# RMSNorm with SiLU on one core: gamma's row fetched as eight transfers of 1 KB in place of one of 8 KB

## The chip, the cores and the metric

The kernel runs on one NeuronCore of a Trainium2 chip. The metric is device time in microseconds; three runs of the kernel before gave 316.78 to 316.95 with a median of 316.93. Durations below come from one profiled execution of it. PE is the matrix engine, DVE the vector engine, ACT the scalar engine, SP the engine that only issues transfers here; "ACTq" and "SPq" are the instruction queues of ACT and SP where they issue a DMA.

## The reference

For x of 8 x 1024 x 2048 float32 (8192 rows of 2048), gamma of 2048 and eps = 1e-5:

```
rms = sqrt(mean(x**2, axis=-1) + eps)
out = gamma * x / rms
out = out * (1 / (1 + exp(-out)))
```

## The kernel before

The 8192 rows are cut into 16 blocks of 512 rows. A block is one SBUF tile `xt` of 128 partitions x 8192 float32 (4 MB): each partition holds J = 4 rows of 2048, which lie next to each other in memory. The pool holds six such tiles (BUFS = 6), and a block is computed in place: it is loaded into its tile, squared, scaled, put through SiLU and stored from the same tile. So load b + 6 needs the tile of block b to be stored.

Loads are issued by ACT (line 54) and stores by SP (line 102), one transfer of 4 MB each. The program order on each engine is written out by hand (`manual_schedule`). Per block b:

- squares: sums of squares of the four rows, one or two of them on ACT (line 65, `squares_scalar`), the others on DVE (line 73, `squares_vector`, whose elementwise output goes to the PSUM tile `junk_v` and is not used);
- `root` on ACT (line 82) gives the rms and `invert` on DVE (line 87) its reciprocal;
- `multiply` on DVE (line 92): four instructions, x * rstd * g;
- `silu` on ACT (line 98): two instructions, then the store.

The squares of block b + 1 stand between the multiply and the SiLU of block b, or before both, according to b. The load of block b + 3 (from block 6 on) is issued by ACT behind the first squares of block b + 1. The last block is multiplied by gamma alone (line 155), and its SiLU takes the reciprocal as a scale (line 157).

Before the loop stands the start-up (lines 106 to 118), which the change touches. ACT issues load 0. DVE fills `ones` and `eps_t`. ACT runs one small activation (line 109). SP issues the fetch of gamma into row 0 of the tile `g` (line 110). PE spreads that row over the 128 partitions: four matmuls (line 113) of a row of ones by 512 columns of g write `junk_v` in PSUM. ACT issues load 1. DVE copies `junk_v` to `g` (line 115). ACT then reads one column of `junk_v` (line 116, which makes ACT wait for DVE's copy), and only behind that, in ACT's program order, are loads 2 to 5 issued (lines 117 and 118). The squares of block 0 come next on both engines.

Of the kernel before, what the change touches and what calls it, by code (L numbers as in the profile page):

```python
# [1 line left out]

# [4 lines left out]

ACT = mybir.ActivationFunctionType
ALU = mybir.AluOpType


@with_exitstack
def kernel(
    ctx: ExitStack,
    tc: tile.TileContext,
    x: bass.AP,
    gamma: bass.AP,
    eps: bass.AP,
    out: bass.AP,
):  # L20

    nc = tc.nc
    P = nc.NUM_PARTITIONS
    f32 = mybir.dt.float32
    x2 = x.flatten_outer_dims()
    o2 = out.flatten_outer_dims()  # L30
    n, d = x2.shape
    J = 4
    BUFS = 6
    nblk = n // (P * J)
    xb = x2.rearrange("(b p j) d -> b p (j d)", p=P, j=J)
    ob = o2.rearrange("(b p j) d -> b p (j d)", p=P, j=J)

    singles = ctx.enter_context(tc.tile_pool(name="singles", bufs=1))
    pool = ctx.enter_context(tc.tile_pool(name="pool", bufs=BUFS))
    small = ctx.enter_context(tc.tile_pool(name="small", bufs=2))  # L40
    psum = ctx.enter_context(tc.tile_pool(name="psum", bufs=1, space=bass.MemoryType.PSUM))

    Q = 4
    w = d // Q
    g = singles.tile([P, d], f32)
    eps_t = singles.tile([P, 1], f32)
    ones = singles.tile([P, P], f32)
    junk_a = psum.tile([P, d], f32, name="junk_a")
    junk_v = psum.tile([P, d], f32, name="junk_v")
    blocks, sss, rmss, rstds = {}, {}, {}, {}  # L50

    def load(b):
        xt = pool.tile([P, J * d], f32, name="xt")
        nc.scalar.dma_start(out=xt, in_=xb[b])  # L54
        blocks[b] = xt

    def row(b, j):
        return blocks[b][:, j * d:(j + 1) * d]

    def squares_scalar(b, loads=()):  # L60


        sss[b] = small.tile([P, J], f32, name="ss")
        for j in range(share(b)):
            nc.scalar.activation(out=junk_a, in_=row(b, j), func=ACT.Square,  # L65
                                 accum_out=sss[b][:, j:j + 1])
            if j == 0:
                for s in loads:
                    load(s)

    def squares_vector(b):
        for j in range(share(b), J):
            nc.vector.tensor_tensor_reduce(  # L73
                out=junk_v, in0=row(b, j), in1=row(b, j), scale=1.0, scalar=0.0,
                op0=ALU.mult, op1=ALU.add, accum_out=sss[b][:, j:j + 1])

    def share(b):
        return 1 if 4 <= b <= 12 and b % 2 == 0 else 2

    def root(b):  # L80
        rms = small.tile([P, J], f32, name="rms")
        nc.scalar.activation(out=rms, in_=sss.pop(b), func=ACT.Sqrt, scale=1.0 / d, bias=eps_t)  # L82
        rmss[b] = rms

    def invert(b):
        rstd = small.tile([P, J], f32, name="rstd")
        nc.vector.reciprocal(out=rstd, in_=rmss.pop(b))  # L87
        rstds[b] = rstd

    def multiply(b):  # L90
        for j in range(J):
            nc.vector.scalar_tensor_tensor(out=row(b, j), in0=row(b, j), scalar=rstds[b][:, j:j + 1],  # L92
                                           in1=g, op0=ALU.mult, op1=ALU.mult)

    def silu(b):
        for h in range(0, J, 2):
            cols = slice(h * d, (h + 2) * d)
            nc.scalar.activation(out=blocks[b][:, cols], in_=blocks[b][:, cols], func=ACT.Silu)  # L98
        store(b)

    def store(b):
        nc.sync.dma_start(out=ob[b], in_=blocks[b])

    with tc.manual_schedule():

        load(0)
        nc.vector.memset(ones, 1.0)  # L107
        nc.vector.memset(eps_t, float(eps))
        nc.scalar.activation(out=junk_a[:, 0:1], in_=ones[:, 0:1], func=ACT.Square)  # L109
        nc.sync.dma_start(out=g[0:1, :], in_=bass.AP(tensor=gamma.tensor, offset=gamma.offset, ap=[[d, 1], [1, d]]))  # L110
        for c in range(Q):
            cols = slice(c * w, (c + 1) * w)
            nc.tensor.matmul(junk_v[:, cols], ones[0:1, :], g[0:1, cols], start=True, stop=True)  # L113
        load(1)
        nc.vector.tensor_copy(out=g, in_=junk_v)  # L115
        nc.scalar.copy(out=junk_a[:, 0:1], in_=junk_v[:, d - 1:d])  # L116
        for b in range(2, BUFS):
            load(b)

        last = nblk - 1
        SOON = 3
        squares_scalar(0)
        squares_vector(0)
        root(0)
        invert(0)
        for b in range(last):
            loads = [b + 3] if BUFS <= b + 3 < nblk else []
            if b < SOON:  # L130
                multiply(b)
                squares_scalar(b + 1, loads)
                silu(b)
                squares_vector(b + 1)
                root(b + 1)
            elif b < last - 1:
                squares_scalar(b + 1, loads)
                squares_vector(b + 1)
                root(b + 1)
                multiply(b)  # L140
                silu(b)
            else:
                multiply(b)
                squares_scalar(b + 1)
                silu(b)
                squares_vector(b + 1)
                root(b + 1)
            if b + 1 < last:
                invert(b + 1)


        for j in range(J):
            if j == J // 2:
                invert(last)
            nc.vector.tensor_mul(out=row(last, j), in0=row(last, j), in1=g)  # L155
        for j in range(J):
            nc.scalar.activation(out=row(last, j), in_=row(last, j), func=ACT.Silu,  # L157
                                 scale=rstds[last][:, j:j + 1])
        store(last)


# [1 line left out]
_INS = ['x', 'gamma', 'eps']  # L163
_OUTS = [((8, 1024, 2048), 'float32')]

_NUMBERS = {'eps': 9.999999747378752e-06}


# [26 lines left out]
```

## Time and profile before

| what | value |
|---|---|
| median of 3 runs | 316.93 us (316.78 to 316.95) |
| span of the profiled execution, first to last instruction | 315.1 us |
| time around the span in that execution | not given by its page; the median of the runs is 1.8 us above the span |
| DVE busy | 235.3 us, 75% of the span |
| ACT busy | 213.9 us, 68% |
| PE busy | 7.2 us, 2% |
| bytes moved | 134.24 MB, 426 GB/s over the span |
| granted PE clock | 1.000 |
| load, from issue to landing, median of 16 | 38.7 us |
| store, the same | 29.0 us |

The span is the time from the first to the last instruction of the execution. The page cuts it into 40 slices of 7.9 us and gives for each the busy tenths of every engine and of the 16 DMA engines that all transfers share. A row of the timeline has the start, the duration, the engine, the line, the operation, its tiles and in brackets the idle time of the engine ahead of it and what ended that. Besides, the trace has a record of each DMA packet with its start, duration, queue and bytes. In these records the loads are on queue q10, and the stores and gamma on q1.

### The profile page before, as it was taken

How to read it: one execution, taken by the hardware profiler on the slowest of the kernel's cores; microseconds unless marked ns; L12 is line 12 of the kernel's file. 1: busy time of each engine (PE TensorE's matmuls, PEld its weight loads, DVE VectorE, ACT ScalarE, POOL GpSimd, SP SyncE). 2: the span in 40 equal slices, each digit the busy share in tenths (PEclk: the TensorE clock that was granted, in tenths of full speed). 3: DMA queues.
4: the chain of work that ended last, by engine and by line, in shares of the span. 5: the costliest groups of instructions: out<-in, count | busy, mean ns of one | idle time of the engine just before them, and what ended most of it. 6: DMA issues, size and time to landing. Idle time of an engine off the chain costs nothing.

```text
span 315.1 us, 439 instructions
## 1 busy us (share of the span) xinstructions
PE 7.2 (2%) x8; PEld 2.5 (1%) x8; DVE 235.3 (75%) x157; ACT 213.9 (68%) x137; POOL 0.2 (0%) x4
## 2 busy tenths in 40 slices
PE   6200000000000000000000000000000000000000
PEld 2000000000000000000000000000000000000000
DVE  0679697979895695957969489593995939999600
ACT  1269998972799258682687827877278768779910
POOL 0000000000000000000000000000000000000000
DMA  8999999999999999999999999999999999999997
GB/s 334 412 453 416 383 458 408 462 403 462 403 459 408 454 412 458 408 462 403 462 403 462 408 458 408 458 408 458 416 449 416 449 416 449 428 437 428 437 428 308
DMA packets 4613, 134.24 MB, mean 426 GB/s; under 512 B 514, under 2 KB 514, under 8 KB 514
## 3 DMA queue, kind: packets, MB, share of 16 engines
q10 hardware_dynamic: 2304, 67.11, 49.8%
q1 hardware_dynamic: 2306, 67.12, 49.3%
q14 instruction: 3, 0.02, 0.0%
HBM read 67.12 MB, written 67.11 MB: 426 GB/s over the span
## 4 chain that ended last, share of the span: by engine, by line
DMA 68%; DVE 14%; ACT 11%; issue 1%; ACTq 1%; DVEq 0%
DMA xt<-in_x_dram 68%; DVE xt L92 9%; DVE junk_v L73 5%; ACT xt L98 4%; ACT junk_a L65 3%; ACT xt L157 2%; ACT L82 1%; ACTq L190 1%; ACT L157 0%; ACT L98 0%; ACT rms L82 0%; DVE ss L73 0%; ACTq L54 0%; DVE rstd L87 0%; ACT L109 0%
## 5 line engine op out<-in xcount | busy, mean ns | idle before, releaser
L92 DVE SCALAR_TENSOR_TENSOR xt<-xt,rstd,g 128x2048 f32<-128x2048 f32 x60 | 137.0, 2346 | 0.1
L98 ACT ACTIVATE xt<-xt 128x4096 f32<-128x4096 f32 x30 | 108.3, 3615 | 27.4 <-DVE xt L92 27.4
L73 DVE CUSTOM_DVE_ANT_0 junk_v<-xt 128x2048 f32<-128x2048 f32 x37 | 85.1, 2299 | 42.9 <-DMA xt<-in_x_dram 42.2
L65 ACT ACTIVATE junk_a<-xt 128x2048 f32<-128x2048 f32 x27 | 50.7, 1876 | 16.1 <-DMA xt<-in_x_dram 14.0
L82 ACT ACT_TABLE_LOAD x15 | 19.2, 1283 | 26.6 <-DVE ss L73 26.5
L98 ACT ACT_TABLE_LOAD x14 | 18.0, 1283 | 0.2
L115 DVE COPY g<-junk_v 128x2048 f32<-128x2048 f32 x1 | 2.3, 2292 | 9.0 <-PE junk_v L113 9.0
L87 DVE RECIPROCAL rstd<-rms 128x4 f32<-128x4 f32 x16 | 2.7, 172 | 8.4 <-ACT rms L82 8.4
L155 DVE TENSOR_TENSOR xt<-xt,g 128x2048 f32<-128x2048 f32 x4 | 8.9, 2277 | 0.0
L82 ACT ACTIVATE rms<-ss,eps_t 128x4 f32<-128x4 f32 x16 | 4.8, 297 | 5.7 <-DVE ss L73 5.5
L157 ACT ACTIVATE xt<-xt,rstd 128x2048 f32<-128x2048 f32 x4 | 7.7, 1991 | 0.0
L113 PE MATMUL junk_v<-g,ones 1*128 1x512 f32 x8 | 7.2, 1072 | 2.8 <-DMA g<-in_gamma_dram 2.8
L116 ACT COPY junk_a<-junk_v 128x1 f32<-128x1 f32 x1 | 0.1, 144 | 9.8 <-DVE g L115 9.8
L73 DVE DVE_READ_ACCUMULATOR2_ANT ss<- 128x1 f32 x37 | 5.2, 141 | 0.0
L65 ACT ACTIVATION_READ_ACCUMULATOR junk_a<-xt 128x1 f32 x27 | 5.0, 186 | 0.0
L113 PEld LDWEIGHTS junk_v<-g,ones 1*128 1x128 f32 x8 | 2.5, 325 | 5.9 <-issue 5.9
L109 ACT ACT_TABLE_LOAD x1 | 1.3, 1283 | 1.1 <-PEq L176 1.1
L157 ACT ACT_TABLE_LOAD x1 | 1.3, 1283 | 0.0
L107 DVE MEMSET ones<- 128x128 f32 x1 | 0.2, 165 | 0.8 <-PEq L176 0.8
L109 ACT ACTIVATE junk_a<-ones 128x1 f32<-128x1 f32 x1 | 0.2, 174 | 0.0
L176 POOL MEMSET const-bfloat16-1.0<- 128x1 bf16 x1 | 0.1, 103 | 0.0
L176 POOL MEMSET const-uint8-127<- 128x1 uint8 x1 | 0.1, 102 | 0.0
(3 smaller groups left out, 0.3 us busy)
## 6 DMA issues: line engine op xcount, KB each, us to landing
xt<-in_x_dram ACTq DMA_DIRECT2D x16, 4096.0 KB, 38.7
out_dram<-xt SPq DMA_DIRECT2D x16, 4096.0 KB, 29.0
g<-in_gamma_dram SPq DMA_DIRECT2D x1, 8.0 KB
```

The source lines that it names most:

```text
L65: nc.scalar.activation(out=junk_a, in_=row(b, j), func=ACT.Square, accum_out=sss[b][:, j:j + 1])
L73: nc.vector.tensor_tensor_reduce(out=junk_v, in0=row(b, j), in1=row(b, j), scale=1.0, scalar=0.0, op0=ALU.mult, op1=ALU.add, accum_out=sss ...
L82: nc.scalar.activation(out=rms, in_=sss.pop(b), func=ACT.Sqrt, scale=1.0 / d, bias=eps_t)
L87: nc.vector.reciprocal(out=rstd, in_=rmss.pop(b))
L92: nc.vector.scalar_tensor_tensor(out=row(b, j), in0=row(b, j), scalar=rstds[b][:, j:j + 1], in1=g, op0=ALU.mult, op1=ALU.mult)
L98: nc.scalar.activation(out=blocks[b][:, cols], in_=blocks[b][:, cols], func=ACT.Silu)
L109: nc.scalar.activation(out=junk_a[:, 0:1], in_=ones[:, 0:1], func=ACT.Square)
L113: nc.tensor.matmul(junk_v[:, cols], ones[0:1, :], g[0:1, cols], start=True, stop=True)
L115: nc.vector.tensor_copy(out=g, in_=junk_v)
L155: nc.vector.tensor_mul(out=row(last, j), in0=row(last, j), in1=g)
L157: nc.scalar.activation(out=row(last, j), in_=row(last, j), func=ACT.Silu, scale=rstds[last][:, j:j + 1])
L190: with _tile.TileContext(nc) as tc:
```

## The change

Gamma's row is still fetched into the same place by SP, at the same place in the program, but in eight transfers of 256 elements (1 KB) each. There were 33 transfers in all (16 loads, 16 stores, one of gamma), and there are now 40. Nothing else differs in the source. Line numbers behind line 110 move by three: the matmuls are at line 116, the copy at 118, ACT's read at 119, the last block's multiply at 158 and its SiLU at 160.

```diff
         nc.scalar.activation(out=junk_a[:, 0:1], in_=ones[:, 0:1], func=ACT.Square)
-        nc.sync.dma_start(out=g[0:1, :], in_=bass.AP(tensor=gamma.tensor, offset=gamma.offset, ap=[[d, 1], [1, d]]))
+        piece = d // 8
+        for at in range(0, d, piece):
+            nc.sync.dma_start(out=g[0:1, at:at + piece],
+                              in_=bass.AP(tensor=gamma.tensor, offset=gamma.offset + at, ap=[[d, 1], [1, piece]]))
         for c in range(Q):
             cols = slice(c * w, (c + 1) * w)
             nc.tensor.matmul(junk_v[:, cols], ones[0:1, :], g[0:1, cols], start=True, stop=True)
```

In the built program, each transfer signals its end on one of eight completion semaphores, which are given out in turn; the issue of a transfer whose semaphore was given out before waits until the earlier transfer has signalled. The order of the built program shows these waits: before, load 0 has number 0 and gamma number 1; after, load 0 has number 0, the eight pieces have 1 to 7 and then 0, and load 1 has number 1.

## The prediction

> **What bounds the kernel now.** I read the slices and the DMA queues of the page first, then the chain that ended last, then the timeline of the first 25 us, then the trace's packet records.
>
> ```profile
> DVE  0679697979895695957969489593995939999600
> ACT  1269998972799258682687827877278768779910
> ...
> DMA  8999999999999999999999999999999999999997
> ```
> ```profile
> q10 hardware_dynamic: 2304, 67.11, 49.8%
> q1 hardware_dynamic: 2306, 67.12, 49.3%
> ```
> The reader should see that DVE and ACT have holes in every block and the DMA engines have none. Loads (q10) are 16 x 144 packets: 128 rows of 32 KB and one completion packet of 4 bytes from each of 16 engines. Stores (q1) are as many, and the two packets left over are all of gamma: one of 8 KB and its completion, on one engine. In the packet records each engine is never without a packet from 1.8-2.8 us to its last one at 313.11-313.95 us. So only two things move the end: time in which an engine has nothing queued, and packets added to an engine. Work on DVE, ACT and PE counts only if it delays an issue until the queues are dry.
>
> The start is where that can happen:
>
> ```profile
> 0.73 0.38 ACTq L54 DMA_DIRECT2D xt<-in_x_dram  x1
> 0.73 0.33 SPq L110 DMA_DIRECT2D g<-in_gamma_dram  x1
> ...
> 2.78 7.16 PE L113 MATMUL junk_v<-g,ones 1*128 1x512 f32 x8 [2.78 <-DMA g<-in_gamma_dram]
> ...
> 9.97 2.29 DVE L115 COPY g<-junk_v 128x2048 f32<-128x2048 f32 x1 [8.98 <-PE junk_v L113]
> 12.36 0.14 ACT L116 COPY junk_a<-junk_v 128x1 f32<-128x1 f32 x1 [9.75 <-DVE g L115]
> 12.38 1.81 ACTq L54 DMA_DIRECT2D xt<-in_x_dram  x4
> 13.08 2.30 DVE L73 CUSTOM_DVE_ANT_0 junk_v<-xt 128x2048 f32<-128x2048 f32 x1 [0.82 <-DMA xt<-in_x_dram]
> ...
> 22.68 1.88 ACT L65 ACTIVATE junk_a<-xt 128x2048 f32<-128x2048 f32 x1 [2.75 <-DMA xt<-in_x_dram]
> ```
> Gamma lands, PE spreads it (four matmuls), DVE copies it to SBUF, ACT reads junk_v, and only behind that ACT instruction do loads 2 to 5 go out, at 12.38. Load 0 is seen landed at about 13.0 (DVE's row), load 1 at 22.66 (ACT's row). The records put load 1's last completions at 21.66 to 22.30 on the 16 engines. Loads 2 to 5 thus go out some ten microseconds before the engines need them. That is the cover of the whole gamma chain.
>
> **Part 1: eight issues and their completion semaphores.** The order of the built program shows what the diff doesn't: all transfers take eight completion semaphores in turn, and a transfer whose semaphore is still out waits for the one that had it. Load 0 has number 0, the pieces g0 to g6 have 1 to 7, and the eighth, g7, has 0 again: **SP issues g7 only after load 0 has landed, about 13.0 us.** Behind it on SP stand the 16 stores, the first issued at 35.18: nothing there is held up. Load 1 now waits for g0, loads 2 to 5 for g1 to g4; load 1 then goes out near 2.8 instead of 1.21, while load 0 keeps the engines busy to 12.0-12.6: no cost. Matmul k waits for its own two pieces, so the first three run earlier; the last needs g7. DVE's copy needs all. Later transfers keep the same relations, since the numbers are only shifted by seven (mod 8).
>
> **Part 2: how the pieces travel.** I take it that all pieces use the one engine that carried gamma's two packets. It also carries a sixteenth of every load: eight packets of 32 KB, 1.2094 us each. How two queues share an engine is seen in its records at 56-66 us (start us, duration ns, queue, bytes):
>
> ```
> 55.502 1213 q1  32768
> 56.711 1213 q10 32768
> 57.921    9 q1      4
> 57.927 1213 q10 32768
> 59.136 1213 q1  32768
> ```
> One packet from each queue in turn, and the 4-byte completion takes a turn like a row. A small packet itself costs next to nothing (9 ns), but **each gamma packet waits out a load packet**. Seven pieces after the first have 14 packets, 14 turns.
>
> Working it on that engine: before, gamma's packet began at 1.641 (706 ns), its completion at 2.343, the engine's first load packet at 2.349; its load packets ended at 4.13, then every 1.2094: the eighth at 12.60, load 1's at 13.8, 15.0, 16.2, 17.4, 18.65, 19.9, with load 0's own completion taking one turn at 12.60. If g0 slips through like gamma before and g1 gets its turn after the first load packet, then g6's completion stands behind load 1's third (16.2), g7's data behind the fourth (17.4), g7's completion behind the fifth: 18.65. (g7, issued at 13.05, is ready at about 14.0, as gamma began 0.91 after its issue; so the queue, not the semaphore, is late.) If an engine has already taken a second load packet when g1 comes, all shift by one: 19.86. For that speaks the first store: issued at 35.18, on every engine two more load packets began (36.2 and 37.9) before its first at 39.6. For the earlier end speaks that in steady state there is one. The trace can't decide; I take the middle, 19.25.
>
> From the completion to the issue of load 2, by rows: PE sees it 0.41 later (2.343 to 2.75); one matmul is two records at a spacing of 0.854 plus 0.33 of drain, 2.04; DVE's copy 0.02 + 2.29; ACT's issue 0.12. Sum 4.88. So load 2 is issued at 24.1 (23.5 to 24.7) instead of 12.38. From load 0: issue 0.73, and the slowest first packet on an engine without gamma ended at 4.03, so in effect that engine worked from 4.03 - 1.21 = 2.82, 2.09 after the issue. The engines restart at 26.2 (25.6 to 26.8), where the slowest had work without a break past 22.30. **The engines stand dry for 3.9 us (3.3 to 4.5).**
>
> **Part 3: after that.** An idle DMA engine is never paid back: queues are full to the end. The compute runs about 11 us late at first (copy end 23.9 for 12.26), so store 0 goes out near 44-45 for 35.18. Until then the loads run alone, so no bandwidth is lost; loads are then ahead by about half a block more. Load 6, issued at 66.72 now, would be issued near 77, and load 5, landed at 85.3 now, would land near 82: the load queue stays fed, and stores would fill it otherwise. At the end store 15 is issued at 300.91 while store 14's packets end at 303.4-304.3, 3 us of cover; with the stores further behind the loads it grows. The compute lag closes, as DVE waits 42.2 us for loads over the run. The seven added completions cost 7 x 9 ns, nothing. Sum: span 315.1 + 3.9 = 319.0. The page gives no time around the span; the runs' median, 316.93, is 1.8 above it, and I keep that: **320.8**.
>
> A rule to weigh. The records show turns of one packet of 32 KB. The Trainium skill, "DMA: Bandwidth & Descriptors", section "Queues, rings and completion order", says that an engine drains a packet of typically 9 to 17 descriptors from one queue before it switches. By that, the pieces would wait for a load's whole share of nine at a time: g1 to g6 at 12.6, g7 behind load 1 at 22.3, and the sum would be about +7 us, 324. The rows at 56-66 us contradict it here, so it is not in the sum.
>
> **Rivals.**
> 1. *The pieces don't cost turns* (several small packets pass between two load packets, or an early burst gets ahead of load 0). Then only the semaphore counts: g7 issued at 13.05, and gamma's whole way (0.73 to 2.75) takes 2.0: seen at 15.1, with one or two load packets ahead 16.3 to 17.5. Load 2 would be issued at 19.5 to 22.0, the restart at 21.6 to 24.1 against 22.30: 0 to +1.8 us, 316.9 to 318.7. For it: in the first rows gamma's completion did follow its data with no load between. Against it: no load packet is seen to start there before 2.349, and in the shared stretch completions do wait.
> 2. *Each piece costs more than two turns*, or a small packet stalls its engine. At the first store two packets took 3.4 us instead of 2.4 on every engine; one such stall puts +5.5, 322.4; two load packets per gamma packet would put the last piece past 35 us and the sum near +20.
> 3. *Faster.* The engine that carries gamma got its first load packet late, behind 0.7 us of gamma's 8 KB, and it is the engine whose load 0 and load 1 end last (12.60, 22.30). With 1 KB in front it starts earlier. This decides only if load 2 is issued before 22.30 - 2.09 = 20.2, that is if g7 is seen before 15.7. The last two engines end at 313.95 and 313.80, so it gives 0.15 us, and up to 1.1 if the microsecond lost at the first store also goes: 315.8 to 316.8.
>
> **How the numbers follow.** Forecast, turns and a dry stretch of 2.5 to 5.0 us: 0.64, at 320.8, own range 319.4 to 321.9. Rival 1: 0.24, half of it within 0.2% (0.63 us, about what a measurement of this kernel can tell from no change). Rival 2: 0.07. Rival 3: 0.05. So slower 0.64 + 0.12 + 0.07 = 0.83, same 0.12, faster 0.05. The range reaches down into rival 1 and up to one stall: 317.1 to 322.6; it leaves out rival 3, the far part of 2 and part of the unchanged cases.
>
> **What would show it.** Right: eight issues at L112, the last after 13 us; the last matmul near 20 and the copy from 21.6 to 23.9; the four loads issued near 24; slices of about 22 to 26 us with the DMA nearly idle and the rest full; DVE's first squares near 24 instead of 13.08; span near 319. Wrong: a copy ending before 20 with full DMA slices (rival 1), or the copy late but the end unmoved, which would mean that the queues are not what sets the end.

## The result

| | kernel before | changed kernel |
|---|---|---|
| median | 316.85 us (316.78 to 316.95, 5 runs) | 321.59 us (321.29 to 323.27, 5 runs) |
| ratio | | 1.0156 (95% interval 1.0145 to 1.0167) |
| span of the profiled execution | 315.1 us | 319.5 us |
| that execution's own time | | 321.33 us |

Slower by 4.7 us; the forecast was 320.8 with a range of 317.1 to 322.6. Times are medians; ratios are estimated from all the runs counted and need not be the quotient of the medians. (Runs more than 1.5% above the fastest of the same kernel are left out of the ratios here and below: one of the four with two and a half copies, and two of the four with the first piece on ACT, whose profiled execution was one of them, so that only its ratio and its first 25 us are used.)

The timeline of the changed kernel's start, in the same columns as before: start, duration, engine, line, operation, tiles, and in brackets the idle time ahead and what ended it.

```profile
0.72 12.61 SPq L112 DMA_DIRECT2D g<-in_gamma_dram  x8
0.72 0.38 ACTq L54 DMA_DIRECT2D xt<-in_x_dram  x1
...
2.00 0.33 ACTq L54 DMA_DIRECT2D xt<-in_x_dram  x1
...
6.61 2.04 PE L116 MATMUL junk_v<-g,ones 1*128 1x512 f32 x2 [6.61 <-DMA g<-in_gamma_dram]
...
11.56 2.04 PE L116 MATMUL junk_v<-g,ones 1*128 1x512 f32 x2 [2.90 <-DMA g<-in_gamma_dram]
...
15.29 2.04 PE L116 MATMUL junk_v<-g,ones 1*128 1x512 f32 x2 [1.69 <-DMA g<-in_gamma_dram]
...
20.14 2.07 PE L116 MATMUL junk_v<-g,ones 1*128 1x512 f32 x2 [2.82 <-DMA g<-in_gamma_dram]
22.25 2.29 DVE L118 COPY g<-junk_v 128x2048 f32<-128x2048 f32 x1 [21.26 <-DMA xt<-in_x_dram]
24.64 0.14 ACT L119 COPY junk_a<-junk_v 128x1 f32<-128x1 f32 x1 [22.03 <-DVE g L118]
24.67 1.87 ACTq L54 DMA_DIRECT2D xt<-in_x_dram  x4
```

Each matmul waits for its own two pieces, 5 us, 4 us and 5 us apart. The copy stands under the name of a load, but the row above it shows what it really waited for: the fourth matmul, which ends at 22.21. Loads 2 to 5 go out at 24.67 instead of 12.38. SP's row holds eight issues over 12.61 us; its list of waits says where that time is:

```profile
SPq L112 <- DMA xt<-in_x_dram: 10.2, 1, 10.2
```

That is the eighth piece, held until load 0 landed. What the DMA engines did meanwhile is in the two-microsecond windows of the same execution (window and length, busy time and instructions of each engine, granted clock, mean share of the DMA engines, GB/s; a packet counts whole in the window in which it starts, so the shares of single windows scatter about 1 where the engines are full). First the kernel before, then the changed kernel:

```profile
20.00:22.00 2.00, 0.00 (x0) 0.00 (x0) 1.96 (x2) 0.00 (x0) 0.00 (x0) 1.00 0.91 393
22.00:24.00 2.00, 0.00 (x0) 0.00 (x0) 2.00 (x2) 1.32 (x1) 0.00 (x0) 1.00 0.91 393
24.00:26.00 2.00, 0.00 (x0) 0.00 (x0) 2.00 (x2) 1.97 (x3) 0.00 (x0) 1.00 1.21 524
```

```profile
18.00:20.00 2.00, 0.00 (x0) 0.00 (x0) 0.00 (x0) 0.00 (x0) 0.00 (x0) 1.00 1.21 525
20.00:22.00 2.00, 1.86 (x2) 0.50 (x2) 0.00 (x0) 0.00 (x0) 0.00 (x0) 1.00 0.61 262
22.00:24.00 2.00, 0.22 (x1) 0.00 (x0) 1.75 (x1) 0.00 (x0) 0.00 (x0) 1.00 0.00 0
24.00:26.00 2.00, 0.00 (x0) 0.00 (x0) 1.73 (x2) 0.14 (x1) 0.00 (x0) 1.00 0.79 213
```

From 22 to 24 us the sixteen DMA engines start nothing but load 1's last completions (to 22.42). After these they are dry: nothing is queued for them. The packet records give the loss: load 1's last completion comes at 22.42, load 2's at 36.66, 14.24 us apart, where one load takes 9.68 on an engine that is never dry. That is a loss of **4.56 us**. On average an engine has no packet for 3.8 us of it (22.04 to 25.83); most of the rest is load 2's first packets, which take 1.6 to 2.3 us instead of 1.21. Afterwards the engines are full again, and their last packet comes at 318.38 instead of 313.95, 4.43 later.

The turns are in the records of the engine that carries gamma (start us, duration ns, queue, bytes):

```
 1.633   51 q1   1024      first piece
 1.680    9 q1      4
 4.880   46 q1   1024      second piece
 6.131    9 q1      4
 7.347   46 q1   1024
 7.389 1213 q10 32768
 8.598    9 q1      4
 8.604 1213 q10 32768
 9.814   46 q1   1024
...
18.478   46 q1   1024      eighth piece
19.730    9 q1      4
```

A piece of 1 KB takes 46 ns and its completion 9 ns; from the second piece on each waits 1.2 us for a load packet, except that at 12.3 us load 0's own completion, of 9 ns, takes the place of one. By the Trainium skill, "DMA: Bandwidth & Descriptors", section "Queues, rings and completion order", an engine drains a packet of typically 9 to 17 descriptors of one queue before it turns to the next. These rows contradict that, if a record is taken as one descriptor: the turn is one record, a 32 KB row or a 4-byte completion alike.

### The profile page after: what moved, and what is told of

Its sections match the earlier page's. It is cut to its first block, busy times and chain, and to the rows that moved or that the text cites. A ratio compares the mean times of both kernels' runs of the same rounds, so it can differ in the third digit from the quotient of the medians.

```text
span 319.5 us, 451 instructions
## 1 busy us (share of the span) xinstructions
PE 8.2 (3%) x8; PEld 2.0 (1%) x8; DVE 235.0 (74%) x157; ACT 213.5 (67%) x137; POOL 0.2 (0%) x4
## 4 chain that ended last, share of the span: by engine, by line
DMA 51%; DVE 23%; ACT 13%; issue 4%; ACTq 1%; DVEq 0%
DMA xt<-in_x_dram 28%; DMA out_dram<-xt 24%; DVE xt L92 14%; DVE junk_v L73 9%; ACT xt L98 5%; ACT junk_a L65 3%; ACT L82 2%; ACT xt L160 2%; DVE g L118 1%; ACTq L54 1%; ACTq L193 1%; ACT rms L82 1%; ACT L160 0%; ACT L98 0%; ACT L109 0%
## 5 line engine op out<-in xcount | busy, mean ns | idle before, releaser
L92 DVE SCALAR_TENSOR_TENSOR xt<-xt,rstd,g 128x2048 f32<-128x2048 f32 x60 | 137.1, 2347 | 0.1
L82 ACT ACT_TABLE_LOAD x15 | 19.2, 1283 | 20.6 <-DVE ss L73 20.5
L116 PE MATMUL junk_v<-g,ones 1*128 1x512 f32 x8 | 8.2, 1125 | 14.0 <-DMA g<-in_gamma_dram 14.0
```

## The experiments

The theory at this point: gamma's packets take turns with load packets (a turn is the wait for one packet of the other queue); the last piece is late by fourteen turns; so load 2 is late; and the time in which no queue has work is the whole cost. Rivals: a fixed price for each transfer; the eighth piece's wait for load 0; and the late start of the computation itself.

### How many pieces: four and six

```diff
-        piece = d // 8
+        piece = d // 4
```

> Gamma in four transfers of 2 KB. Turns theory (each gamma packet behind the first piece waits out one load packet of 1.21 us, and only the time in which the DMA queues are dry moves the end): the three later pieces have six turns; the last completion stands where the fourth one stands in the profile of the changed kernel, at 11.07 us; load 2 is issued 4.94 later (19.73 to 24.67 there), at 16.0, and load 1's packets last to 22.4, so nothing is dry: 316.9, as before, within 0.4, although gamma lands eight us later than as one transfer. Rival, a price per transfer (4.74 us for seven added ones, 0.68 each, wherever it falls): three added, 318.9.

Measured: 317.31 us, ratio 1.0011 (1.0002 to 1.0021). The last completion stands at 11.37 and load 2 goes out at 16.28. Gamma lands nine microseconds late for 0.35 us.

```diff
-        piece = d // 8
-        for at in range(0, d, piece):
+        cuts = [0, 256, 512, 768, 1024, 1536, 2048]
+        for at, to in zip(cuts, cuts[1:]):
             ...
```

> Gamma in six transfers (four of 1 KB, two of 2 KB). No piece and not load 1 waits for load 0; load 2 does, which has landed by then. Turns theory: ten turns, the last completion at 14.80 us (the sixth one's place in the profile of the changed kernel), load 2 issued at 19.7, first packets in effect 1.6 to 2.3 later (24.67 to 26.27 to 26.98 there), 21.3 to 22.0, against load 1's end at 21.8 to 22.4: just not dry, 316.9 to 317.2. Price per transfer: five added, 320.2.

Measured: 318.74 us, ratio 1.0064 (1.0044 to 1.0084). The start went as the theory says (last completion 15.09, load 2 issued at 20.01, no engine dry), but the time is 1.8 us up, between the two expectations. A fixed price for a transfer is out (three cost 0.35, five 1.8, seven 4.7), and so is the dry queue as the only cost.

### The wait for load 0 taken away

The first piece is issued by ACT ahead of load 0. The completion numbers then fall so that the eighth piece waits for the first.

```diff
+        fetch(0, nc.scalar)
         load(0)
         ...
-        for at in range(0, d, piece):
+        for at in range(piece, d, piece):
```

> Eight pieces of 1 KB, but the first is issued by ACT ahead of load 0, so that the semaphore of the eighth was the first piece's and not load 0's; all seven on SP are issued at once. Six pieces take turns behind SP's first. Turns theory: the last completion where the seventh piece's stands in the changed kernel, 17.26 us, perhaps 0.4 later since load 0 goes out behind one more issue; load 2 issued at 22.2 to 22.6, dry some 2.1 us instead of 4.6, plus up to 0.4 for the late start: 319.0 to 319.6. Semaphore theory (the eighth piece is late because it waits for load 0 at 13 us): without that wait gamma is complete by about 5 us, nothing is dry, 316.9 to 317.4.

Measured: 318.88 and 321.72 us, ratio 1.0103 (1.0051 to 1.0156). SP's and PE's rows of its first 20 us:

```profile
0.73 2.21 SPq L109 DMA_DIRECT2D g<-in_gamma_dram  x7
...
14.66 2.07 PE L121 MATMUL junk_v<-g,ones 1*128 1x512 f32 x2 [1.61 <-DMA g<-in_gamma_dram]
```

All seven issues are out by 2.94 us, and still the last matmul can't start before 14.66: nothing but turns lies between, and the semaphore theory (about 5 us) falls. The turns were fewer than expected, since load 0 went out later and two pieces got ahead of it. Load 2 went out at 19.18, no engine was dry, and yet the kernel is 1% slower. So here too is a cost that the dry queue doesn't explain.

### Eight pieces without a dry queue

```diff
         nc.vector.tensor_copy(out=g, in_=junk_v)
-        nc.scalar.copy(out=junk_a[:, 0:1], in_=junk_v[:, d - 1:d])
         for b in range(2, BUFS):
             load(b)
+        nc.scalar.copy(out=junk_a[:, 0:1], in_=junk_v[:, d - 1:d])
```

> Eight pieces as in the changed kernel, but ACT issues loads 2 to 5 ahead of its read of junk_v instead of behind it. Gamma still completes near 19.8 us and DVE's copy still ends near 24.6. Turns theory with the dry queue as the only cost: the loads are issued by 13 us at the latest (each waits for the completion of one of the first pieces), the queues are never dry, 316.9 within 0.4. Rival, the late start of the computation costs by itself: 321.6 as the changed kernel, or most of the 4.7 us of it.

Measured: 321.56 us, ratio 1.0134 (1.0109 to 1.0158). Its windows at the places where the changed kernel was dry, and at the end:

```profile
20.00:22.00 2.00, 1.84 (x2) 0.50 (x2) 0.00 (x0) 0.00 (x0) 0.00 (x0) 1.00 0.87 377
22.00:24.00 2.00, 0.22 (x1) 0.00 (x0) 1.74 (x1) 0.00 (x0) 0.00 (x0) 1.00 0.95 410
24.00:26.00 2.00, 0.00 (x0) 0.00 (x0) 1.73 (x2) 1.32 (x2) 0.00 (x0) 1.00 1.21 524
```
```profile
312.00:314.00 2.00, 0.00 (x0) 0.00 (x0) 0.00 (x0) 0.00 (x0) 0.00 (x0) 1.00 1.02 442
314.00:316.00 2.00, 0.00 (x0) 0.00 (x0) 0.00 (x0) 0.00 (x0) 0.00 (x0) 1.00 0.68 295
316.00:318.00 2.00, 0.00 (x0) 0.00 (x0) 0.00 (x0) 0.00 (x0) 0.00 (x0) 1.00 0.15 66
```

The hole at 22 to 24 us is gone, and the time is about the same as with it. My expectation was wrong by the whole 4.7 us. The end shows another form of loss: the work thins out over four microseconds. The first DMA engine ends at 314.64, 0.7 us after the last one of the kernel before, and the last at 318.79; in the kernel before they ended within 0.84 us of each other. The packet records show why: between 90 and 270 us, 146 load packets and 24 store packets take 1.3 to 2.2 us instead of 1.21, on some engines more than on others, the load packets mostly among the first few of a load. Next to nothing of that is in the changed kernel (3 of its 2,381 packets between 90 and 270 us took over 1.3 us; here 170 of 2,342).

### Late without any piece

Gamma is fetched in one transfer, and DVE repeats its copy of junk_v to g, 2.33 us each time.

```diff
-        nc.vector.tensor_copy(out=g, in_=junk_v)
+        for _ in range(6):
+            nc.vector.tensor_copy(out=g, in_=junk_v)
```

> Gamma in one transfer as in the kernel before, but DVE makes its copy of junk_v to g six times instead of once, so that ACT's read and loads 2 to 5 come 11.7 us later (5 x 2.33), at about 24.0, as late as with eight pieces (24.67). Lateness theory (it matters only when load 2 goes out, not that the pieces are many): the engines stand dry from load 1's end at 22.3 to about 26.2, span 319.0, time 320.8 to 321.3. Rival, the sixteen small packets and their completions cost by themselves: 316.9, or clearly under 320.

Measured: 321.51 us, ratio 1.0161 (1.0123 to 1.0198). Load 2 goes out at 24.06, and the windows have the same hole:

```profile
22.00:24.00 2.00, 0.00 (x0) 0.00 (x0) 1.93 (x1) 0.00 (x0) 0.00 (x0) 1.00 0.00 0
24.00:26.00 2.00, 0.00 (x0) 0.00 (x0) 1.78 (x1) 0.14 (x1) 0.00 (x0) 1.00 0.92 262
```

One transfer made late costs as much as eight pieces. The small packets by themselves cost nothing that shows.

The same with ACT's read behind the loads, as above:

> One transfer of gamma, six copies on DVE as in the kernel with five added ones, and ACT issues loads 2 to 5 ahead of its read. No queue is dry at the start, and the computation starts 11.7 us late. Theory of the late stores (a late store 0 makes the turns of loads and stores from one block to the next fall together, and load packets then take 1.3 to 2.0 us instead of 1.21): like the run of eight pieces with the loads ahead, 320.5 to 321.8, and its DMA engines end far apart (there 314.6 to 318.8). Theory of the dry queue alone, with the eight pieces to blame for that run: 316.9.

Measured: 322.01 us, ratio 1.0164 (1.0149 to 1.0179); DMA ends at 315.16 to 318.42. Stretched packets again (those over 1.3 us), without pieces.

Four copies in place of six, ACT's read ahead of the loads as in the kernel before:

> One transfer of gamma, four copies on DVE instead of one: the read and loads 2 to 5 come 7.0 us later, at about 19.4, ahead of the 20.2 from which the queue would be dry. Store 0 should go out near 40 instead of 35.18 (40.56 with six pieces, where load 2 went out at 20.01), and the stores pass from block to block about 2 us behind the loads. Theory of the late stores: 318 to 319, like six pieces (318.74), without any piece. Dry queue alone: 316.9 to 317.2.

Measured: 322.84 us, ratio 1.0178 (1.0161 to 1.0195), slower than expected and the slowest so far, with no engine dry, load 2 out at 19.39 and store 0 at 40.03. Half a copy less:

```diff
-        nc.vector.tensor_copy(out=g, in_=junk_v)
+        for _ in range(3):
+            nc.vector.tensor_copy(out=g, in_=junk_v)
+        nc.vector.tensor_copy(out=g[:, 0:d // 2], in_=junk_v[:, 0:d // 2])
```

> As the run with three added copies, but with two and a half: 5.9 us later. Store 0 near 38.8; each us that it is later lets the loads gain two us of turns, so the ends of a load and of a store (7.2 us apart before, 3.3 with four pieces, 2 to 4 the other way with six) should fall together within a microsecond. Theory of the late stores: at least as slow as with three added copies, 318.5 or more, perhaps the slowest without a dry queue. Dry queue alone: 316.9.

Measured: 319.08 us (319.00 to 320.10), ratio 1.0077 (1.0059 to 1.0095), with store 0 at 39.05. That it would be slower than three copies was wrong.

### Only store 0 late

All late runs share one thing besides the late computation: store 0 is late, and with it the place where the stores stand against the loads. From store 0 on, each engine alternates one load packet and one store packet, so the distance between the end of a load and the end of a store nearly keeps its value over the run. To move that distance and nothing else, the kernel before gets a copy of one column of block 0 onto itself, behind the first, second or third multiply of block 1 (`j == 1` below, 2 and 3 in the other two), and store 0 waits for it. Gamma comes in one transfer.

```diff
+    def late_store():
+        nc.vector.tensor_copy(out=blocks[0][:, 0:1], in_=blocks[0][:, 0:1])
+        store(0)
+
     def multiply(b):
         for j in range(J):
+            if b == 1 and j == 1:
+                late_store()
             ...
-        store(b)
+        if b > 0:
+            store(b)
```

> The kernel before, gamma in one transfer and nothing late, but the issue of store 0 alone is held until DVE's first multiply of block 1 is done, about 39.4 us instead of 35.18. The end of a store then stands some 1 us behind the end of a load (7.2 ahead before, each us of lateness of store 0 moves it by two). Theory of the phase (load packets are stretched when the two streams pass from block to block within some four us of each other, stores behind): slower although no engine computes later, 318.5 to 322. Rival, the late computation is what costs in the runs with added copies: 316.9, since here only one store moves.

Measured: 322.95 us, ratio 1.0191 (1.0174 to 1.0208). Its start, to compare with the rows of the kernel before:

```profile
36.96 2.35 DVE L98 SCALAR_TENSOR_TENSOR xt<-xt,rstd,g 128x2048 f32<-128x2048 f32 x1
...
39.23 0.15 DVE L91 COPY xt<-xt 128x1 f32<-128x1 f32 x1
39.30 6.87 DVE L98 SCALAR_TENSOR_TENSOR xt<-xt,rstd,g 128x2048 f32<-128x2048 f32 x3
39.46 10.71 SPq L109 DMA_DIRECT2D out_dram<-xt  x2
```

The computation is where it was (37.01 in the kernel before), store 1 goes out at 49.84 (49.83 before), and only store 0 is 4.3 us late. That costs 6 us. The same kernel once more:

> The same kernel as the run with store 0 at 39.4, once more for a look at the spread from run to run: same times as there.

Measured: 321.07 us in its one run, 0.6 us below the lowest of the four before. The next two push store 0 further:

> Store 0 held until the second multiply of block 1 is done, about 41.7 us. The end of a store should stand 5 to 6 us behind the end of a load, about as in the kernel with eight pieces (4.9), where load packets kept their 1.21 us. Theory of the phase: quick again although store 0 is later than in the run before this one, 316.9 to 317.6. Theory that the cost grows with the lateness of store 0: slower than the run with store 0 at 39.4, 323 or more.

Measured: 317.09 us, ratio 1.0008 (0.9999 to 1.0018), with store 0 at 41.69. The ends stood 7.2 us apart, farther than expected.

> Store 0 held until the third multiply of block 1 is done, about 44.0 us: store ends some 10 us behind load ends, the farthest from them. Theory of the phase: 316.9 to 317.3, its load packets at 1.21 us. Theory that the cost grows with the lateness of store 0: slower still than with 41.7.

Measured: 316.93 us, ratio 0.9999 (0.9990 to 1.0009), with store 0 at 44.04. The nearest store end stood 7.3 us ahead of a load end, the place that it has in the kernel before.

The end of the run with store 0 at 39.46, and of the one with store 0 at 44.04, in the same windows:

```profile
312.00:314.00 2.00, 0.00 (x0) 0.00 (x0) 0.00 (x0) 0.00 (x0) 0.00 (x0) 1.00 0.99 426
314.00:316.00 2.00, 0.00 (x0) 0.00 (x0) 0.00 (x0) 0.00 (x0) 0.00 (x0) 1.00 0.53 229
316.00:318.00 2.00, 0.00 (x0) 0.00 (x0) 0.00 (x0) 0.00 (x0) 0.00 (x0) 1.00 0.12 49
```
```profile
312.00:314.00 2.00, 0.00 (x0) 0.00 (x0) 0.00 (x0) 0.00 (x0) 0.00 (x0) 1.00 0.27 115
314.00:316.00 2.00, 0.00 (x0) 0.00 (x0) 0.00 (x0) 0.00 (x0) 0.00 (x0) 1.00 0.00 0
316.00:318.00 2.00, 0.00 (x0) 0.00 (x0) 0.00 (x0) 0.00 (x0) 0.00 (x0) 1.00 0.00 0
```

Later by 4.3 us costs 6 us, later by 8.9 us costs nothing. So the cost isn't lateness but the place. The table orders the runs by the distance from the end of load 10 to the nearest end of a store (medians over the engines, from the completion packets; the last row belongs with the first); "stretched" counts packets of 32 KB, loads and stores, over 1.3 us among those that start between 90 and 270 us.

| run | distance us | stretched | last DMA packet, 16 engines | ratio |
|---|---|---|---|---|
| kernel before | -7.3 | 1 of 2,380 | 313.11 to 313.95 | 1 |
| four pieces | -2.6 | 2 of 2,375 | 313.15 to 314.00 | 1.0011 |
| two and a half copies added | 0.8 | 177 of 2,352 | 314.19 to 317.11 | 1.0077 |
| store 0 at 39.46 | 2.4 | 146 of 2,347 | 314.36 to 318.70 | 1.0191 |
| the same kernel once more | 2.4 | 140 of 2,339 | 314.91 to 318.09 | 321.07 us, one run |
| eight pieces, loads ahead | 2.5 | 170 of 2,342 | 314.64 to 318.79 | 1.0134 |
| five copies added, loads ahead | 2.5 | 155 of 2,336 | 315.16 to 318.42 | 1.0164 |
| three copies added | 4.0 | 113 of 2,348 | 314.59 to 320.53 | 1.0178 |
| six pieces | 4.8 | 14 of 2,381 | 312.95 to 315.49 | 1.0064 |
| five copies added | 4.8 | 2 of 2,377 | 316.95 to 317.88 | 1.0161, dry |
| eight pieces (the change) | 4.8 | 3 of 2,381 | 317.45 to 318.38 | 1.0156, dry |
| store 0 at 41.69 | 7.2 | 2 of 2,381 | 313.27 to 314.79 | 1.0008 |
| store 0 at 44.04 | -7.3 | 2 of 2,381 | 312.95 to 313.85 | 0.9999 |

Two of these medians, 0.8 and 4.0, mix engines. Followed engine by engine, the distances lie near 0.0, 2.4 or 4.8 us, two turns apart: with two and a half copies eight engines stand at 0.0 and eight at 2.4, with three copies nine stand at 2.4 and seven at 4.8. At 0.0 nearly all the stretched packets are stores; at 2.4 in the same run nine in ten are loads.

Six pieces hold the sharpest test, within one execution. Fourteen of its engines stand at 4.8 us and have no stretched packet or one; the two others stand at 2.4 to 2.6 us, over most of the run, and hold 24 of the 25 packets over 1.26 us that start from 50 us on. Those two end at 314.98 and 315.49, the others by 313.54. But an engine's own distance isn't all: with three copies the seven engines at 4.8 us hold 30 of the 113 stretched packets, mostly at the same moments as the nine others (near 123, 162, 201 and 240 us).

The records also close the sum. In the six rows from two and a half copies to three copies the engines have next to no idle time between 45 and 300 us (on average 0.06 us at most beyond the kernel before). What the 32 KB packets take beyond 1.213 us each, from 10 us on, is 2.4 to 3.2 us per engine more than in the kernel before, and the mean of the sixteen ends is 2.5 to 3.3 us later, row by row the same within 0.1 us. The rest is that the engines share it unevenly: the last one ends 0.8 to 3.9 us behind that mean, against 0.5 before. With six pieces the mean hardly moves (0.03 us), and the two engines alone make the kernel late.

## Why the prediction was right

**The completion numbers.** Right: the eighth issue came behind load 0, its wait was 10.2 us, and nothing behind it on SP was held up. Load 1 went out at 2.00, not 2.8, at no cost either way. That this wait isn't what makes the piece late was also right, and the run with the first piece on ACT shows it.

**The turns.** Right: the two possible ends of the last completion were 18.65 and 19.86, and it came at 19.73. I took the middle where the trace couldn't decide; the later end is the true one, because the gamma engine had taken two load packets (to 3.67 and to 4.88) before the second piece got its turn. That is the row of the first store, which I had cited for it.

**From the completion to the issue.** 4.88 expected; 4.94 measured (19.73 to 24.67).

**The dry engines.** 3.9 was the middle of 3.3 to 4.5; 4.56 measured, within 0.1 us the sum for the later turn. With it the forecast would have been 321.5, against a median of 321.59 and 321.33 for the profiled execution. The mis-sized term is this one, by 0.7 us.

**The rest of the run.** "Only two things move the end", time in which an engine has nothing queued and packets added to an engine, was wrong as a rule. It holds for the changed kernel, whose load and store ends lie 4.8 us apart, but a third thing moves the end by as much: packets that are stretched in the runs where those ends lie 0 to 2.5 us apart on half of the engines or more. I had store 0 going out near 44-45 (45.35) and thought only of bandwidth and cover, not of where the two streams would meet. That the changed kernel stood at 4.8 us was luck for the forecast: eight pieces at 2.5 us cost as much with no engine dry.

**Rival 1**, the pieces without turns, fell with the records. Its time, 316.9 to 318.7, was worked out from dry time alone; load 2 out at 19.2 to 20.0 gave 318.7 to 322.8 in three kernels with no engine dry. **Rival 2**: the extra load packet before the second piece is a small part of it; no stall of an engine showed. **Rival 3**: the gamma engine did start earlier (first load packet done at 3.67 instead of 4.13), and with the queue dry later it decided nothing.

What is shown: the pieces make load 2 late, and the late load leaves the engines dry and costs them 4.56 us; the same lateness without pieces gives the same time. What is not: that closing the hole would give the time back. It did not, because the loads then gained on the stores and stood at 2.5 us. Both changes to the start alter that distance, so the two costs can't be removed one by one in this kernel.

## What to carry to other kernels

Two queues shared the DMA engines here, and a transfer waited in turns and not in bytes: each small packet and each completion stood behind one packet of the other queue (1.21 us for 46 and 9 ns of its own). So split a small fetch only where nothing else is queued, or not at all. Ask next what is issued behind its arrival, and compare that moment with the time at which the queues run out; four pieces fit into that cover here (0.35 us), eight didn't (4.7 us). For many small transfers the Trainium skill ("DMA: Bandwidth & Descriptors", section "Rules for kernel authors") says to coalesce: "under 64 KB you're paying mostly overhead". That has the right sign, but no run here shows a fixed price per transfer.

In a kernel bound by its transfers, look also at where loads and stores end against each other: moving one store by 4 us cost 6 us here, and by 9 us nothing.

## What was not expected of the hardware

- Stretched packets. In the runs where the end of a store stood 0 to 2.5 us behind the end of a load on half of the engines or more, 113 to 177 packets took 1.3 to 2.5 us instead of 1.21, loads mostly at 2.4 us and stores at 0.0, and the engines drifted apart to 5.9 us at the end. With all or nearly all engines at 4.8, 7.2, -7.3 or -2.6 us, next to nothing of it shows. Why is open: the passing from one transfer to the next in both queues within about two turns, or the memory addresses that loads and stores touch at that distance, would both fit, and no run tells them apart. That in the run with three copies engines at 4.8 us were stretched at the same moments as those at 2.4 speaks for something that the engines share.
- The first packets after an empty queue are slow: load 2's first packets in the changed kernel took 1.6 to 2.3 us each, as load 0's did at the start (1.6 to 2.2), against 1.21 later.
- A small packet in a busy engine is nearly free by itself: 46 ns for 1 KB, 9 ns for a completion.
